# A planner's prices: engine times and GpSimd's hold in the simulated schedule of a two-block transformer kernel

## The chip, the cores and the metric

One core of a Trainium2 chip runs the whole program. The metric is the device time of one execution in microseconds; of the kernel before it is 4151.16 us, the median of three runs (4149.66 to 4156.11).

## The reference

Everything is float32, one sequence of 1024 tokens of width 1024, and a context of 256 tokens. The reference runs two different blocks one after the other:

```python
def reference(...):
    x = first_block(x, c, ctx, c_ctx, ...)   # two hybrid layers, then an RMS norm
    return second_block(x, p_2, ...)         # one layer of another kind
```

A layer of the first block normalizes and modulates the input, projects it (`h @ w_in`), and mixes three branches: attention with a latent key-value projection (6 heads), attention with grouped keys (6 heads, 2 key heads), both over the sequence and the context, and a gated depthwise convolution of 31 taps with a layer norm. The branches are gated, joined and multiplied by `w_out`. The second layer does not compute the context's output.

The second block computes a projection of 7896 columns; a gated linear attention in chunks; an indexer that scores keys, takes the 256 best of each query, and a sparse latent attention over them; their gated mix; a feed-forward part with a convolution of three taps; and a gated embedding. Three layer norms stand between.

## The kernel before

The kernel writes all of this as a list of small operations on tiles of 128 partitions by up to 512 columns, features on the partitions and tokens on the columns, in chunks of 512, 512 and 256 (context) tokens. For precision most operands are split in two halves of a reduced format: `hi` is a cast of the value (`copy`, line 293 of VectorE or line 284 of ACT), `lo` the rest (`lo`, a `tensor_tensor` subtraction, line 325 on VectorE or 327 on GpSimd), and a product is three matmuls (line 384): hi by hi, hi by lo and lo by hi. So nearly every matrix that TensorE reads has first passed through one cast and one subtraction.

Each operation (`Op`) has in `alts` the engines that can run it, each with a price in microseconds: `t` TensorE, `a` ACT, `v` VectorE, `p` GpSimd, `d` a DMA. Many casts can go to `a` or `v`, many subtractions, sums and products to `v` or `p`; the rest has one engine. GpSimd cannot read PSUM, so only operations on SBUF have `p`. `Plan.schedule` then simulates the engines with these prices: at each moment an engine that is free takes the ready operation of the lowest number (`pr`), and an operation with two engines is refused by the dearer one when the cheaper engine's remaining work, 0.6 us for each operation that stands ready there (at most 12), and its own price sum up to less than the price on the dearer one. The finish of an operation, its price and a fixed delay (`LAT`) make its readers ready. Buffers are handed out in the same simulation: 89 tiles of 128x512 in SBUF (`pg`), 8 PSUM banks (`ps`) and a few others. `Plan.merge` interleaves two lists of operations by the sum of their `t` prices.

What comes out is an order for each engine, which is emitted as it stands (`emit`). On the chip every engine works off its queue in this order; the simulation's times are gone, and an instruction that waits holds up all that follow it on its engine.

The stages in their order are: embedding, norm and modulation (to about 100 us), projections and convolution of layer 0, its two attentions, its output; the same for layer 1; indexer and scores; gated linear attention with the top-k search on VectorE beside it; its projection; the sparse attention; its projections; the feed-forward part; the gated embedding with the last layer norm.

The helpers with prices are `c_act` and `act` (ACT), `copy`, `c_v`, `c_p`, `tt` (sum, product, subtraction), `stt` and `ts` (VectorE with scalars), `scale`, `red` (maximum along a row), `mm` and `tr` (TensorE). For 512 columns of SBUF the old prices are 0.520 us on ACT, 0.600 for `tt` on VectorE and 1.225 on GpSimd, 0.660 for `stt`, 0.334 for a cast on VectorE, 0.216 for a matmul.

Of the kernel before, what the change touches and what calls it, by code (L numbers as in the profile page):

```python
# [4 lines left out]
F32 = mybir.dt.float32  # L5
# [110 lines left out]
class View:  # L116


    __slots__ = ("buf", "ap", "ops", "key")
# [42 lines left out]


class Op:
    __slots__ = ("alts", "reads", "writes", "emit", "idx", "succ", "npred", "allocs", "table", "bufs", "tag", "pr", "late")


BASIC = ("Copy", "Identity", "Square", "Abs", "Relu")
# [4 lines left out]
class Plan:  # L173
# [37 lines left out]
    def op(self, alts, reads, writes, emit, table=None):  # L211
        o = Op()
        o.alts = alts
        o.reads = [x for x in reads if isinstance(x, View)]
        o.writes = [x for x in writes if isinstance(x, View)]
        o.emit = emit
        o.table = table
        o.tag = self.tag
        o.late = self.late
        self.cur.append(o)  # L220
        return o
# [37 lines left out]
        return out  # L259

    def c_act(self, n, src, extra=0):
        return (n * 0.833 + (52 if isinstance(src, View) and src.psum else 93) + extra) / 1000

    def act(self, out, in_, func, bias=None, scale=1.0, accum=None, alts=None):
        nc = self.nc
# [31 lines left out]
    def copy(self, out, in_, engs="av"):  # L297
        a = {}
        n = out.n
        if "v" in engs:  # L300
            a["v"] = (n * (1.04 if in_.psum else 0.52) + 68) / 1000
        if "a" in engs:
            return self.act(out, in_, "Copy", alts=a)
        return self.op(a, [in_], [out], lambda e: self._copy(e, out, in_))
# [2 lines left out]
        return {"v": self.nc.vector, "p": self.nc.gpsimd}[e]  # L307

    def c_v(self, n, ex=0):
        return (n * 1.04 + 68 + ex) / 1000  # L310

    def c_p(self, n):
        return (n * 2.1 + 150) / 1000

    def tt(self, out, in0, in1, op, engs="v"):
        o = getattr(OP, op)
# [23 lines left out]
    def ts(self, out, in0, s1, s2, op0, op1=None, accum=None):  # L340
        o0 = getattr(OP, op0)
        k = {} if op1 is None else {"op1": getattr(OP, op1)}

        def emit(e):
            if accum is not None:
                k["accum_out"] = real(accum)
            self.nc.vector.tensor_scalar(out=real(out), in0=real(in0), scalar1=real(s1), scalar2=real(s2), op0=o0, **k)  # L347

        return self.op({"v": (out.n * (1.04 if in0.psum or accum is not None else 0.52) + 130 + (127 if accum is not None else 0)) / 1000},
                       [in0, s1, s2], [out, accum], emit)  # L350

    def scale(self, out, in_, col):

        n = out.n

        def emit(e):
            if e == "a":
                self.nc.scalar.activation(real(out), real(in_), AF.Copy, scale=real(col))
            else:
                self.nc.vector.tensor_scalar(out=real(out), in0=real(in_), scalar1=real(col), scalar2=None, op0=OP.mult)  # L360

        return self.op({"v": (n * (1.04 if in_.psum else 0.52) + 130) / 1000, "a": self.c_act(n, in_, 93)},
                       [in_, col], [out], emit)

    def red(self, out, in_, op="max"):
# [13 lines left out]

    def mm(self, out, lhsT, rhs, start, stop, cost=None):  # L380
        n = rhs.n
        c = cost or max(n * 1.676 if rhs.ap.dtype == F32 or n < 256 else n * 0.4219, 60) / 1000
        return self.op({"t": c}, [lhsT, rhs] + ([] if start else [out]), [out],
                       lambda e: self.nc.tensor.matmul(real(out), lhsT=real(lhsT), rhs=real(rhs), start=start, stop=stop))  # L384

    def tr(self, out, in_, ident):
        return self.op({"t": 0.109}, [in_, ident], [out],
                       lambda e: self.nc.tensor.transpose(real(out), real(in_), real(ident)))  # L388

    def dma(self, out, in_, cost=None):  # L390
# [10 lines left out]
    def schedule(self, window=1500, dwindow=1200, boost=0, queue=0.25, verbose=False):  # L401
# [8 lines left out]
        for o in ops:  # L410
            preds = set()
            bufs = {}
# [110 lines left out]
        while len(order) < N:  # L523
            progress = False
            for e in engs:
                while busy[e] <= now + 1e-9:
# [41 lines left out]
                    issued[o.idx] = True  # L568
                    progress = True
                    c = o.alts[e]  # L570
                    pre = None
                    if e == "a" and o.table is not None and o.table != table:
                        pre = o.table
# [1467 lines left out]
```

## Time and profile before

| | |
|---|---|
| median of 3 runs | 4151.16 us (4149.66 to 4156.11) |
| the profiled execution: time, span | 4150.0 us, 4148.1 us |
| TensorE busy, matmuls | 3908.4 us (94%), 18536 |
| VectorE busy, instructions | 3306.3 us (80%), 5640 |
| ACT busy, instructions | 2036.4 us (49%), 3969 |
| GpSimd busy, instructions | 1430.2 us (34%), 1257 |
| mean granted TensorE clock | 0.980 |

In the profile PE is TensorE's matmul, PEld its weight load, DVE VectorE, ACT ScalarE, POOL GpSimd. Matmuls overlap each other, so that a busy TensorE is not one at its peak. The mean length of an instruction is from its start to its end, also where the next one has started before that.

### The profile page before, as it was taken

What the parts mean: (1) busy time and instruction counts of PE and PEld (TensorE: products, weight loads), DVE (VectorE), ACT (ScalarE), POOL (GpSimd) and SP (SyncE); (2) the same over time, 40 slices, a digit from 0 to 9 for tenths busy, and PEclk for the clock granted to TensorE, in tenths of its full rate; (3) what the DMA queues carried; (4) which work ended last, traced back from release to release, by engine and by line L of the source; (5) the groups of instructions that cost most, each with busy time, mean ns of one, the idle gap of its engine ahead of it and who ended that gap; (6) DMA issues with size and microseconds to landing.
All of it is one profiled execution on the core that took longest, in us unless ns stands there. A gap on an engine that the chain in (4) does not pass through costs nothing. (4 is left out here: it accounts for less than half of the span.)

```text
span 4148.1 us, 54250 instructions
## 1 busy us (share of the span) xinstructions
PE 3908.4 (94%) x18536; PEld 3153.5 (76%) x18536; DVE 3306.3 (80%) x5640; ACT 2036.4 (49%) x3969; POOL 1430.2 (34%) x1257
## 2 busy tenths in 40 slices
PE   7989998989989998999999999999999999999988
PEld 4768766667877776778878878888878788888867
DVE  8995899997896789985999996388886865455588
ACT  5244576774334566763545551366663432222245
POOL 4542455663142344552223441011132411121153
PEclk8999999999999999999999999999999999999998
DMA  7132211123323110042111142100044411111121
GB/s 254 62 117 72 62 54 53 50 70 114 110 83 99 39 34 26 16 133 94 67 44 54 67 142 77 62 31 30 32 144 152 137 51 49 49 41 46 56 82 57
DMA packets 184981, 311.88 MB, mean 75 GB/s; under 512 B 22912, under 2 KB 46208, under 8 KB 184704
## 3 DMA queue, kind: packets, MB, share of 16 engines
q1 hardware_dynamic: 184704, 308.42, 23.0%
q8 instruction: 146, 2.39, 0.2%
q14 instruction: 131, 1.07, 0.1%
HBM read 237.81 MB, written 62.39 MB: 72 GB/s over the span
## 5 line engine op out<-in xcount | busy, mean ns | idle before, releaser
L384 PE MATMUL ps<-pg,pg 128*128 128x512 f32 (+4 forms) x17200 | 3843.6, 380 | 119.1 <-ACT pg L284 43.5
L384 PEld LDWEIGHTS ps<-pg,pg 128*128 128x128 f32 (+2 forms) x17200 | 3009.0, 190 | 798.5 <-ACT pg L284 72.9
L327 POOL TENSOR_TENSOR pg<-pg,pg 128x512 fp32r<-128x512 f32 (+4 forms) x935 | 1355.7, 1462 | 2338.7 <-ACT pg L284 1301.7
L284 ACT ACTIVATE pg<-pg 128x512 fp32r<-128x512 f32 (+9 forms) x1529 | 875.5, 601 | 893.5 <-DVE pg L335 240.6
L325 DVE TENSOR_TENSOR pg<-pg,pg 128x512 fp32r<-128x512 f32 (+8 forms) x1126 | 956.2, 868 | 218.7 <-ACT pg L284 162.6
L284 ACT ACTIVATE pg<-ps 128x512 f32<-128x512 f32 (+9 forms) x1351 | 686.8, 557 | 801.4 <-PE ps L384 597.4
L325 DVE TENSOR_TENSOR pg<-ps,pg 128x128 fp32r<-128x128 f32 (+9 forms) x690 | 381.3, 567 | 209.2 <-PE ps L384 146.3
L335 DVE SCALAR_TENSOR_TENSOR pg<-ux,c,pg 128x512 f32<-128x512 f32 x416 | 348.7, 867 | 9.6 <-ACT pg L284 2.2
L368 DVE TENSOR_REDUCE sm<-ps 128x1 f32<-128x512 f32 (+1 forms) x492 | 326.1, 679 | 9.6 <-PE ps L384 7.0
L293 DVE CAST pg<-pg 128x512 fp32r<-128x512 f32 (+4 forms) x387 | 226.9, 596 | 72.0 <-ACT pg L284 34.0
L284 ACT ACTIVATE pg<-ps,c 128x512 f32<-128x512 f32 (+1 forms) x182 | 127.3, 708 | 250.0 <-PE ps L384 218.5
L335 DVE SCALAR_TENSOR_TENSOR pg<-pg,c,pg 128x512 f32<-128x512 f32 (+3 forms) x242 | 220.1, 946 | 5.5 <-ACT pg L284 5.2
L388 PE MATMUL ps<-c,pg 128*128 128x128 f32 (+1 forms) x796 | 180.2, 274 | 14.3 <-DVE pg L293 5.8
L293 DVE COPY ux<-ps 128x512 f32<-128x512 f32 x83 | 57.3, 690 | 143.3 <-ACT pg L284 133.6
L1523 DVE MAX8 sm<-ux 128x8 f32<-128x384 f32 (+5 forms) x192 | 168.8, 887 | 3.3
L1524 DVE MATCH_REPLACE8 ux<-sm,ux 128x384 f32<-128x384 f32 (+5 forms) x192 | 167.7, 875 | 0.0
L384 PE MATMUL ps<-pg,c 128*128 128x512 f32 (+3 forms) x196 | 85.2, 502 | 74.9 <-DVE pg L325 28.6
L388 PEld LDWEIGHTS ps<-c,pg 128*128 128x128 f32 (+1 forms) x796 | 107.6, 141 | 40.3 <-issue 6.2
L284 ACT ACTIVATE pg<-pg,sm 128x512 f32<-128x512 f32 (+2 forms) x192 | 116.2, 606 | 11.2 <-DVE sm L347 10.7
L384 PEld LDWEIGHTS ps<-pg,c 128*128 128x128 f32 (+2 forms) x196 | 33.6, 176 | 105.7 <-DVE pg L325 31.6
L671 ACT ACT_TABLE_LOAD x84 | 107.8, 1283 | 1.5
L1778 DVE CUSTOM_DVE_ANT_0 pg<-ps,pg 128x512 f32<-128x512 f32 (+3 forms) x176 | 100.0, 575 | 8.5 <-PE ps L384 6.3
(74 smaller groups left out, 1017.2 us busy)
## 6 DMA issues: line engine op xcount, KB each, us to landing
d<-pg SPq DMA_DIRECT2D x202, 256.0 KB, 2.1
pg<-d SPq DMA_DIRECT2D x178, 256.0 KB, 3.3
pg<-in_w2a SPq DMA_DIRECT2D x108, 256.0 KB, 2.8
pg<-in_wmod SPq DMA_DIRECT2D x96, 256.0 KB, 3.1
pg<-in_wup SPq DMA_DIRECT2D x88, 256.0 KB, 2.7
pg<-in_win SPq DMA_DIRECT2D x80, 256.0 KB, 3.3
pg<-in_wout SPq DMA_DIRECT2D x64, 256.0 KB, 3.3
pg<-in_wdn SPq DMA_DIRECT2D x48, 256.0 KB, 2.7
```

What stands on the lines that cost most here:

```text
L284: nc.scalar.activation(real(out), real(in_), fn, scale=real(scale), **k)
L293: self.nc.vector.tensor_copy(real(out), real(in_))
L325: self.nc.vector.tensor_tensor(out=real(out), in0=real(in0), in1=real(in1), op=o)
L327: self.nc.gpsimd.tensor_tensor(out=real(out), in0=real(in0), in1=real(in1), op=o)
L335: self.nc.vector.scalar_tensor_tensor(out=real(out), in0=real(in0), scalar=real(scalar), in1=real(in1), op0=o0, op1=o1)
L368: lambda e: self.nc.vector.tensor_reduce(out=real(out), in_=real(in_), axis=AX.X, op=o))
L384: lambda e: self.nc.tensor.matmul(real(out), lhsT=real(lhsT), rhs=real(rhs), start=start, stop=stop))
L388: lambda e: self.nc.tensor.transpose(real(out), real(in_), real(ident)))
L671: nc.scalar.preload_act_table_set(pre)
L1523: P.vec(P.c_v(n), [w], [m8], lambda e, m8=m8, w=w: nc.vector.max(real(m8), real(w)))
L1524: P.vec(P.c_v(n), [w, m8], [w], lambda e, m8=m8, w=w: nc.vector.match_replace(real(w), real(m8), real(w), MARK))
L1778: lambda e, p=p, s=s, n=n, m=mk[t, b], a=sm[:, b:b + 1]: nc.vector.tensor_tensor_reduce(out=real(p), in0=real(s[:, 0:n]), in1=real(m), sca ...
```

## The change

The prices are replaced. For 512 columns they become 0.630 us on ACT from SBUF, 0.598 from PSUM, 0.687 for `tt` on VectorE, 1.326 on GpSimd, 0.747 for `stt`, 0.421 for a cast, 0.228 for a matmul; a transpose falls from 0.109 to 0.06. A new flag `dual` marks operations that VectorE can run, that read no PSUM and at least one tile of more than 64 columns of SBUF. When the simulation starts such an operation on VectorE while GpSimd is at work, it adds 0.42 us for each us of GpSimd's remaining work, up to the operation's price over 0.58. The choice between two engines still compares the plain prices. `LAT`, the priorities, the buffers and the operations stay.

```diff
 class Op:
-    __slots__ = ("alts", "reads", "writes", "emit", "idx", "succ", "npred", "allocs", "table", "bufs", "tag", "pr", "late")
+    __slots__ = ("dual", "alts", "reads", "writes", "emit", "idx", "succ", "npred", "allocs", "table", "bufs", "tag", "pr", "late")
...
+        o.dual = "v" in alts and not any(x.psum for x in o.reads) and sum(x.n > 64 for x in o.reads) > 0
...
     def c_act(self, n, src, extra=0):
-        return (n * 0.833 + (52 if isinstance(src, View) and src.psum else 93) + extra) / 1000
+        return (n * 0.836 + (170 if isinstance(src, View) and src.psum else 202) + extra) / 1000
...
-            a["v"] = (n * (1.04 if in_.psum else 0.52) + 68) / 1000
+            a["v"] = (n * (1.04 if in_.psum else 0.52) + 155) / 1000
...
     def c_v(self, n, ex=0):
-        return (n * 1.04 + 68 + ex) / 1000
+        return (n * 1.04 + 155 + ex) / 1000
 
     def c_p(self, n):
-        return (n * 2.1 + 150) / 1000
+        return (n * 2.2 + 200) / 1000
...
-        c = cost or max(n * 1.676 if rhs.ap.dtype == F32 or n < 256 else n * 0.4219, 60) / 1000
+        c = cost or max(n * 1.774 if rhs.ap.dtype == F32 or n < 256 else n * 0.4434 + 1, 60) / 1000
...
     def tr(self, out, in_, ident):
-        return self.op({"t": 0.109}, [in_, ident], [out],
+        return self.op({"t": 0.06}, [in_, ident], [out],
...
                     c = o.alts[e]
+                    if e == "v" and o.dual and busy["p"] > now:
+                        c += 0.42 * min(busy["p"] - now, c / 0.58)
```

`ts` and `scale` on VectorE go from 130 to 190 ns beside the columns in the same way.

The order has the same operations; 4463 of them can run on two engines, and 1371 of these now run on the other. By the numbers of the buffers that they write, 493 go from VectorE to GpSimd and 239 back, 370 from VectorE to ACT and 269 back. In sum VectorE's queue has 4901 operations for 5256, ACT's 3761 for 3660, GpSimd's 1507 for 1253. TensorE's 18512 and the 1400 DMAs are the same in number.

First place: the end of layer 0's attention with grouped keys. VectorE's queue before (in a name like pg2638_10097 the first number is the buffer's and is the same in both kernels, the second counts tiles in the order emitted; pg2638 is the low part of the probabilities pg2636, pg2637 their cast):

```order
L293 CAST pg2637_10072<-pg2636_10034 128x512
L293 CAST pg2641_10082<-pg2640_10048 128x512
L325 TENSOR_TENSOR pg2638_10097<-pg2636_10034,pg2637_10072 128x512
L325 TENSOR_TENSOR pg2642_10107<-pg2640_10048,pg2641_10082 128x512
L293 CAST pg2675_10117<-pg2674_10041 128x256
L325 TENSOR_TENSOR pg2675_10117<-pg2674_10041,pg2675_10117 128x256
L293 CAST pg2649_10128<-pg2648_10068 128x512
L325 TENSOR_TENSOR pg2678_10131<-pg2677_10080,pg2678_10131 128x256
L325 TENSOR_TENSOR pg2650_10146<-pg2648_10068,pg2649_10128 128x512
L293 CAST pg2661_10159<-pg2660_10111 128x512
L325 TENSOR_TENSOR pg2658_10167<-pg2656_10103,pg2657_10154 128x512
L325 TENSOR_TENSOR pg2662_10175<-pg2660_10111,pg2661_10159 128x512
```

and GpSimd's queue now, at the same place:

```order
L329 TENSOR_TENSOR pg2634_10023<-pg2632_9972,pg2633_10009 128x512
L329 TENSOR_TENSOR pg2638_10053<-pg2636_9982,pg2637_10044 128x512
L329 TENSOR_TENSOR pg2642_10070<-pg2640_10000,pg2641_10060 128x512
L329 TENSOR_TENSOR pg2675_10082<-pg2674_10029,pg2675_10082 128x256
L329 TENSOR_TENSOR pg2646_10104<-pg2644_10021,pg2645_10089 128x512
L329 TENSOR_TENSOR pg2678_10107<-pg2677_10042,pg2678_10107 128x256
L329 TENSOR_TENSOR pg2658_10141<-pg2656_10057,pg2657_10117 128x512
L329 TENSOR_TENSOR pg2662_10155<-pg2660_10073,pg2661_10126 128x512
```

Six subtractions of VectorE's run (of 2638, 2642, 2675, 2678, 2658, 2662) stand now on GpSimd, in one row with the two that it had before; the subtraction of 2650 stays on VectorE, and the casts of 2675, 2649 and 2661 went to ACT.

Second place: the last chunk of the gated embedding at the program's end, GpSimd's queue before (pg9707 is the sum of the outputs, pg9708 that of their squares, for the last layer norm; the other rows are products, and from pg9740 on the mean is subtracted):

```order
L327 TENSOR_TENSOR pg9708_39759<-pg9708_39759,pg9715_39765 128x256
L327 TENSOR_TENSOR pg9717_39771<-pg9718_39486,pg9717_39771 128x256
L327 TENSOR_TENSOR pg9725_39851<-pg9726_39555,pg9725_39851 128x256
L327 TENSOR_TENSOR pg9729_39868<-pg9730_39564,pg9729_39868 128x256
L327 TENSOR_TENSOR pg9707_39728<-pg9707_39728,pg9721_39846 128x256
L327 TENSOR_TENSOR pg9707_39728<-pg9707_39728,pg9725_39851 128x256
L327 TENSOR_TENSOR pg9708_39759<-pg9708_39759,pg9731_39911 128x256
```

and now:

```order
L329 TENSOR_TENSOR pg9707_39738<-pg9707_39738,pg9717_39725 128x256
L329 TENSOR_TENSOR pg9707_39738<-pg9707_39738,pg9721_39777 128x256
L329 TENSOR_TENSOR pg9707_39738<-pg9707_39738,pg9725_39820 128x256
L329 TENSOR_TENSOR pg9708_39744<-pg9708_39744,pg9719_39862 128x256
L329 TENSOR_TENSOR pg9708_39744<-pg9708_39744,pg9723_39870 128x256
L329 TENSOR_TENSOR pg9708_39744<-pg9708_39744,pg9727_39877 128x256
L329 TENSOR_TENSOR pg9729_39903<-pg9730_39622,pg9729_39903 128x256
L329 TENSOR_TENSOR pg9737_39929<-pg9738_39637,pg9737_39929 128x256
L329 TENSOR_TENSOR pg9708_39744<-pg9708_39744,pg9731_39932 128x256
L329 TENSOR_TENSOR pg9707_39738<-pg9707_39738,pg9733_39926 128x256
L329 TENSOR_TENSOR pg9707_39738<-pg9707_39738,pg9737_39929 128x256
```

Sums that alternated between VectorE and GpSimd now follow each other on GpSimd.

## Rows read from the trace of the kernel before

**Rows 1.** The page, part 1: busy us of each engine, share of the span, instructions
```profile
PE 3908.4 (94%) x18536; PEld 3153.5 (76%) x18536; DVE 3306.3 (80%) x5640; ACT 2036.4 (49%) x3969; POOL 1430.2 (34%) x1257
```

**Rows 2.** By stretch: start:end, length, then PE, PEld, DVE, ACT, POOL busy (count), PEclk, DMA
```profile
104.00:311.00 207.00, 178.93 (x891) 146.83 (x890) 206.01 (x282) 74.45 (x135) 103.60 (x62) 0.95 0.28 89
415.00:980.00 565.00, 511.04 (x2293) 387.35 (x2291) 533.34 (x815) 387.52 (x750) 331.62 (x286) 0.97 0.20 61
1141.00:1244.00 103.00, 90.75 (x403) 72.37 (x402) 101.69 (x127) 40.13 (x69) 51.56 (x26) 0.95 0.26 84
1340.00:1843.00 503.00, 468.67 (x2014) 353.80 (x2013) 447.92 (x699) 331.63 (x608) 252.14 (x245) 0.98 0.14 43
2017.00:2460.00 443.00, 419.30 (x2372) 362.00 (x2371) 424.61 (x779) 237.39 (x512) 167.15 (x144) 0.98 0.22 74
2460.00:2651.00 191.00, 191.00 (x844) 157.29 (x843) 106.88 (x141) 37.77 (x62) 33.25 (x26) 1.00 0.26 85
3960.00:4148.00 188.00, 150.43 (x786) 126.17 (x784) 166.82 (x229) 90.77 (x161) 90.92 (x67) 0.89 0.19 61
```

**Rows 3.** Timeline, one engine at a time: start, us, instructions of one kind in a row
```profile
147.19 26.57 DVE L335 SCALAR_TENSOR_TENSOR pg<-ux,c,pg 128x512 f32<-128x512 f32 x40
...
522.69 2.18 ACT L284 ACTIVATE pg<-pg 128x512 fp32r<-128x512 f32 x4
...
704.95 1.27 DVE L368 TENSOR_REDUCE sm<-ps 128x1 f32<-128x512 f32 x2
...
3701.80 10.37 PE L384 MATMUL ps<-pg,pg 128*128 128x512 f32 x44 [0.25 <-ACT pg L284]
```

**Rows 4.** Costliest groups, shapes apart: count, busy us, mean ns of one, idle before, releasers
```profile
L327 POOL TENSOR_TENSOR pg<-pg,pg 128x512 fp32r<-128x512 f32 x714 | 1085.7, 1531 | 1659.3 <-ACT pg L284 830.4 <-DVE pg L293 358.5 <-PE ps L384 293.8
L284 ACT ACTIVATE pg<-pg 128x512 fp32r<-128x512 f32 x972 | 591.7, 633 | 565.5 <-PE ps L384 153.0 <-DVE pg L325 141.0 <-DMA pg<-in_wup 49.7
L325 DVE TENSOR_TENSOR pg<-pg,pg 128x512 fp32r<-128x512 f32 x555 | 487.3, 891 | 128.8 <-ACT pg L284 90.7 <-PE ps L384 22.8 <-POOL pg L327 7.0
L335 DVE SCALAR_TENSOR_TENSOR pg<-ux,c,pg 128x512 f32<-128x512 f32 x416 | 348.7, 867 | 9.6 <-ACT pg L284 2.2
L325 DVE TENSOR_TENSOR pg<-pg,pg 128x512 f32<-128x512 f32 x271 | 245.4, 924 | 42.7 <-ACT pg L284 36.4 <-POOL pg L327 2.5
L335 DVE SCALAR_TENSOR_TENSOR pg<-pg,c,pg 128x512 f32<-128x512 f32 x192 | 189.5, 1013 | 5.5 <-ACT pg L284 5.2
L293 DVE CAST pg<-pg 128x512 fp32r<-128x512 f32 x297 | 184.2, 628 | 55.0 <-ACT pg L284 30.6 <-PE ps L384 18.6 <-DMA pg<-in_wout 3.5
L325 DVE TENSOR_TENSOR pg<-ps,pg 128x512 fp32r<-128x512 f32 x152 | 99.1, 684 | 23.6 <-ACT pg L284 23.0
L335 DVE SCALAR_TENSOR_TENSOR pg<-ps,c,pg 128x512 f32<-128x512 f32 x56 | 41.4, 745 | 21.8 <-PE ps L384 21.6
```

**Rows 5.** Timeline, 970 to 981 us: three of VectorE's rows, two of GpSimd's
```profile
970.25 1.40 DVE L325 TENSOR_TENSOR pg<-pg,pg 128x512 fp32r<-128x512 f32 x2
972.59 0.43 DVE L293 CAST pg<-pg 128x512 fp32r<-128x512 f32 x1
975.80 3.59 DVE L325 TENSOR_TENSOR pg<-pg,pg 128x512 fp32r<-128x512 f32 x3 [0.16 <-ACT pg L284]
...
975.38 1.41 POOL L327 TENSOR_TENSOR pg<-pg,pg 128x512 fp32r<-128x512 f32 x1 [1.08 <-ACT pg L284]
977.48 3.04 POOL L327 TENSOR_TENSOR pg<-pg,pg 128x512 fp32r<-128x512 f32 x2 [0.69 <-PE ps L384]
```

**Rows 6.** Waits: engine, line <- whom it waited for, us in total, times, longest
```profile
POOL pg L327 <- ACT pg L284: 1357.9, 308, 70.5
PEld ps L384 <- POOL pg L327: 63.1, 98, 6.3
```

**Rows 7.** Timeline near the end: GpSimd's and VectorE's 256-wide instructions
```profile
4105.21 3.39 POOL L327 TENSOR_TENSOR pg<-pg,pg 128x256 f32<-128x256 f32 x3 [2.04 <-DVE pg L325]
...
4107.09 0.93 DVE L325 TENSOR_TENSOR pg<-pg,pg 128x256 f32<-128x256 f32 x1 [0.62 <-POOL pg L327]
```

More of the change, by code (lines that the diff above doesn't have):

```diff
@@ L347, in emit @@
             self.nc.vector.tensor_scalar(out=real(out), in0=real(in0), scalar1=real(s1), scalar2=real(s2), op0=o0, **k)
-        return self.op({"v": (out.n * (1.04 if in0.psum or accum is not None else 0.52) + 130 + (127 if accum is not None else 0)) / 1000},
+        return self.op({"v": (out.n * (1.04 if in0.psum or accum is not None else 0.52) + 190 + (127 if accum is not None else 0)) / 1000},
                        [in0, s1, s2], [out, accum], emit)
@@ L360, in emit @@
                 self.nc.vector.tensor_scalar(out=real(out), in0=real(in_), scalar1=real(col), scalar2=None, op0=OP.mult)
-        return self.op({"v": (n * (1.04 if in_.psum else 0.52) + 130) / 1000, "a": self.c_act(n, in_, 93)},
+        return self.op({"v": (n * (1.04 if in_.psum else 0.52) + 190) / 1000, "a": self.c_act(n, in_, 93)},
                        [in_, col], [out], emit)
```

## The prediction, made before the changed kernel was run

> **What bounds the kernel now.** I read the page first, then a table by stretch, then single stretches of the timeline. TensorE is busy 3908.4 of 4148.1 us and VectorE 3306.3 [rows 1]; a mean over the program says little, so the table by stretch comes next [rows 2]. There the reader should see two kinds of stretch. In 2460 to 2651 us TensorE is busy all the time at a granted clock of 1.00 and VectorE barely half: nothing that VectorE does matters there. In six others (104 to 311, 415 to 980, 1141 to 1244, 1340 to 1843, 2017 to 2460, 3960 to 4148 us: the convolutions, both layers' attention, the top-k beside the gated linear attention, the end) VectorE is busy 1880 of 2009 us, TensorE idles 190 us (of 240 in the whole span), and the granted clock falls to 0.89 to 0.98. So VectorE's load there sets the time, and what the change does to it decides.
>
> **What the new prices are.** Rows of equal instructions back to back show the time that an engine gives to one [rows 3]: 40 convolution steps on VectorE take 26.57 us, 0.664 each; four ACT copies 2.18 us, so with the last one's full length of 0.63 the others take 0.52; two reductions 1.27 us, 0.60 for the first; 44 matmuls 10.37 us, 0.23 each. The groups [rows 4] give lengths instead: 0.867 for the first (with GpSimd's hold) and 0.633 for the second. An instruction starts some 0.08 to 0.11 us before the one ahead of it has ended. The old prices in the code were 0.660, 0.520, 0.600 and 0.216 us; the new ones are 0.747, 0.630, 0.687 and 0.228. So the new matmul price is right where the old was 5% low; the new prices of VectorE and ACT are lengths, and as the time for which the engine is taken they are 13 to 21% high, where the old were right but for the hold. The Trainium skill, page "Perfetto Trace Analysis", section "Optimizing Scalar/DVE Operations", says the same: profiled latency is about twice the engine-busy overhead, as its second half overlaps with the next instruction; the trace agrees (0.664 against 0.747).
>
> **GpSimd's hold is real.** Two subtractions of 128x512 without GpSimd beside them take 1.40 us; three take 3.59 us where GpSimd runs 0.99 and 1.91 us of that time [rows 5]. Alone they would take 0.60 + 0.60 + 0.69 = 1.89 us, so 1.70 us are lost in 2.90, 0.59 per us of GpSimd at most. Over the whole program: instructions that read SBUF twice, or cast from it, against those that read PSUM (0.684 and 0.745) or a cast alone (0.43) [rows 4, 5]: 555 x 0.207 + 271 x 0.240 + 416 x 0.122 + 192 x 0.268 + 297 x 0.198 = 341 us, over GpSimd's 1430 us busy [rows 1] 0.24 per us at least, as smaller groups are left out. The planner was blind to all this and thought VectorE faster than it is; now it thinks it slower than it is. The Trainium skill ("SBUF", section "Who interferes with whom") says that the loser is blocked for the whole instruction; that would be 1 per us, and the rows show at most 0.59. By its price the load term below would be a loss of 116 us.
>
> **The change, part by part.** Nothing computed changes. By buffer numbers, VectorE loses 355 instructions net, GpSimd gains 254 subtractions and products, ACT 101 copies; 157 and 68 of them lie in the six stretches (13 and 8, 40 and 34, 3 and 5, 30 and 16, 35 and 2, 36 and 3 in their order).
>
> 1. Taken from VectorE there: of the 254, 187 are 512 wide (0.60 us by rows 3), the others mostly 256 wide (0.33, half of the columns): 0.53 in the mean, 157 x 0.53 = 83 us. A cast from SBUF gives back about 0.35 (0.43 less 0.08), 68 x 0.35 = 24. Together 107 us.
>
> 2. Given to GpSimd: 1.531 us for 512 columns [rows 4], 1.13 for 256 (three in 3.39 us) [rows 7], 1.42 in the mean, 157 x 1.42 = 223 us more beside VectorE. The hold on it: 54 us at 0.24, 132 at 0.59. I take 0.33, nearer to the lower end since that one is a mean over the program, but above it since in these stretches GpSimd is busier (332 of 565 us in the longest) [rows 2]: 74 us. VectorE's load falls by 107 - 74 = 33 us; ends 53 less and 25 more. The tail is where it is worst: a sum of 256 columns takes 0.93 us beside GpSimd [rows 7], longer than one of 512 without it, and 36 more go over there, into sums that GpSimd now makes in a row (second place of the order).
>
> 3. Lateness. A low part that GpSimd makes lands after 1.53 instead of 0.89 us, and a matmul may wait for it. TensorE's weight loads wait for GpSimd 98 times, 63.1 us [rows 6], 0.065 us for each of the 972 sums, products and subtractions that the order gives GpSimd; 254 more make 16 us. Part of that falls where VectorE sets the pace anyway: +8, ends 0 and 16. The 101 ACT copies, and four more ACT table loads (85 rows to 89), are hidden: ACT is busy 388 of 565 us in the fullest stretch; were it full, they would cost their 0.52 us each on their chains.
>
> 4. Order. PE's queue is nearly the same stage by stage; inside the units it shifts. In the six stretches VectorE itself idles 2009 - 1880 = 129 us, while TensorE also waits: queues in a fixed order, behind a producer that is later than planned. With the old prices producers were late by the hold, with the new ones they are early by 0.08 to 0.11 us each, and a queue that expects its data late waits less. No row prices this: bounds are half of the 129 us gained, 65, and 40 lost. I take an eighth, 16 us gained, nearer to nothing, since most of what is planned stands as before.
>
> The profiled execution took 4150 us (span 4148.1): 4150 - 33 + 8 - 16 = 4109; the median of the runs lies 1 us above it, so **4110 us**.
>
> **The rivals.**
>
> *Late GpSimd operands (slower).* Prices that are too high for VectorE make the planner send to GpSimd even what a matmul needs next. For: at the first place of the order eight low parts stand in a row on GpSimd, which a matmul reads next. Each is 0.64 us later; the 33 us of step 2 are gone when 52 of the 254 are waited for. Now 1 in 10 is (98 of 972). At 1 in 2, 127 x 0.64 = 81 us: 4150 - 33 - 16 + 81 = 4182; without the gain of step 4 and with the hold's upper end 4256. Against: GpSimd mostly waits for its own inputs (1357.9 us for ACT alone) [rows 6], so it takes things as they come. A sentence of the Trainium skill ("Perfetto Trace Analysis", "Optimizing Scalar/DVE Operations") speaks for this: offloading between GpSimd and VectorE might not help, as they share a port.
>
> *Order was the trouble (a larger gain).* If the matching of plan and chip is what TensorE lacked, half of its 190 us of idle time in the six stretches goes, with the clock behind it: 4150 - 33 - 65 = 4052 or below. For: the clock is under 1.00 in each of them [rows 2]. Against: VectorE is 94 to 99% busy in three, and order does not shorten a full engine.
>
> *Nothing comes of it.* The engine choice changes, but at a hold of 107/223 = 0.48 per us VectorE's load stays, and lateness and order cancel: 4150. For: 0.48 lies between the two ends of rows 4 and 5.
>
> **How the numbers follow.** A measurement of this kernel can tell 0.2%, 8 us, from no change. Forecast (4060 to 4142 us) 0.44, larger gain 0.20, nothing 0.12, slower 0.24. So faster 0.64, same 0.12, slower 0.24. The range goes from 4045, which leaves out some 0.08 of the larger gain, to 4180, which leaves out some 0.11 of the slower case. The forecast's own range is 4060 to 4142.
>
> **What would show it.** Right: VectorE's busy time falls by some 60 to 150 us, GpSimd's rises by about 350, and TensorE's idle time in 415 to 980 and 2017 to 2460 us shrinks while the stretch from 2460 on keeps its length. GpSimd's 128x512 mean stays about 1.5 us. Step 2 is wrong if VectorE's busy time hardly falls or the mean of its 128x512 subtraction rises over 1.0 us; step 3 if TensorE's waits for GpSimd go far over 63 + 16 us; step 4 if TensorE's idle time falls by much more or less than VectorE's load. The last 188 us should not get shorter. The prediction fails as a whole if the stretches that VectorE does not bound change by more than a few us, for then order alone was at work.

## The result, and the profile after

The changed kernel takes 4053.27 us (median of 4 runs, 4049.64 to 4054.66), the kernel before on the same chip 4150.41 us: a ratio of 0.976 [0.975, 0.978], 97 us gained. The forecast was 4110 us. The time lies within the stated range (4045 to 4180 us) but below the forecast's own (4060 to 4142), 1 us from the 4052 us of the rival "Order was the trouble"; how much of that hit is luck is said below.

The page of the changed kernel, part 1, beside [rows 1]:

```profile
span 4052.6 us, 54435 instructions
## 1 busy us (share of the span) xinstructions
PE 3878.6 (96%) x18536; PEld 3138.1 (77%) x18536; DVE 3236.8 (80%) x5285; ACT 2077.8 (51%) x4074; POOL 1755.2 (43%) x1511
```

The span is 95.5 us shorter. TensorE's idle time fell from 239.7 to 174.0 us, which is 65.7 of them; its busy time for the same 18536 matmuls fell by 29.8, while the mean granted clock rose from 0.980 to 0.987. VectorE's busy time fell by 70 and GpSimd's rose by 325, both about as forecast.

The table by stretch of the changed kernel, cut where TensorE has done as many matmuls as at the borders of [rows 2] (columns as there):

```profile
108.00:289.00 181.00, 172.85 (x893) 142.30 (x892) 175.14 (x214) 76.67 (x136) 105.85 (x69) 1.00 0.30 100
391.00:944.00 553.00, 509.05 (x2294) 382.70 (x2293) 509.60 (x737) 396.96 (x779) 377.45 (x321) 0.98 0.21 62
1109.00:1205.00 96.00, 88.35 (x401) 71.33 (x400) 87.61 (x102) 41.23 (x72) 58.32 (x28) 0.96 0.30 94
1295.00:1775.00 480.00, 458.01 (x2014) 351.72 (x2013) 434.94 (x657) 334.26 (x625) 299.77 (x279) 1.00 0.15 47
1948.00:2362.00 414.00, 412.01 (x2371) 359.52 (x2370) 374.31 (x693) 232.44 (x502) 187.22 (x174) 1.00 0.23 76
2362.00:2552.00 190.00, 190.00 (x842) 156.62 (x841) 135.34 (x183) 45.54 (x77) 46.64 (x36) 1.00 0.27 92
3867.00:4053.00 186.00, 147.76 (x785) 123.65 (x783) 170.07 (x189) 97.08 (x168) 138.85 (x103) 0.90 0.19 62
```

The six stretches that the prediction called bound by VectorE (all but the sixth row) take 1910 us instead of 2009: the whole gain. VectorE's load in them falls by 128 us, from 1880 to 1752, though over the whole program only by 70. Outside the six it is busy 59 us longer (1485 us, 1426 before): that work has gone elsewhere in time, not to another engine. Part of it is in the sixth row: VectorE is busy 135 us there, not 107 [rows 2], and the stretch is no longer for it, as TensorE sets its pace.

What moved can be counted. Two views show the rounds of the top-k search (one MAX8 each) in the stretch of the gated linear attention and in the one behind it (the fifth and the sixth row); before:

```profile
L1523 DVE MAX8 sm<-ux 128x8 f32<-128x512 f32 (+4 forms) x158 | 127.8, 817 | 2.4
...
L1523 DVE MAX8 sm<-ux 128x8 f32<-128x1024 f32 (+1 forms) x34 | 41.0, 1212 | 0.8
```

and after the change:

```profile
L1527 DVE MAX8 sm<-ux 128x8 f32<-128x384 f32 (+4 forms) x142 | 109.5, 783 | 0.8
...
L1527 DVE MAX8 sm<-ux 128x8 f32<-128x1024 f32 (+1 forms) x50 | 57.4, 1170 | 0.4
```

Sixteen rounds, 18 us of MAX8 and about as much for the replacement that follows each, left the full stretch for one with room. The steps of the first convolution did the same: 171 of them lie in the first row's stretch before, 128 after, and right behind it VectorE is busy 92 of 102 us, where it was busy 60 of 104.

The costliest groups of the changed kernel, shapes apart, of GpSimd and VectorE, and the largest waits of TensorE's weight loads:

```profile
L329 POOL TENSOR_TENSOR pg<-pg,pg 128x512 fp32r<-128x512 f32 x862 | 1294.8, 1517 | 1443.5 <-ACT pg L286 801.5 <-PE ps L386 287.6 <-DVE pg L295 235.3
...
L327 DVE TENSOR_TENSOR pg<-pg,pg 128x512 fp32r<-128x512 f32 x407 | 415.8, 1032 | 89.9 <-ACT pg L286 56.9 <-PE ps L386 19.8 <-POOL pg L329 9.0
L337 DVE SCALAR_TENSOR_TENSOR pg<-ux,c,pg 128x512 f32<-128x512 f32 x416 | 362.6, 898 | 22.2 <-ACT pg L286 13.9 <-POOL pg L329 0.9
...
L327 DVE TENSOR_TENSOR pg<-pg,pg 128x512 f32<-128x512 f32 x232 | 228.6, 1003 | 32.4 <-ACT pg L286 27.2 <-DMA pg<-pg 2.0
L337 DVE SCALAR_TENSOR_TENSOR pg<-pg,c,pg 128x512 f32<-128x512 f32 x192 | 204.8, 1094 | 7.7 <-ACT pg L286 7.6
L295 DVE CAST pg<-pg 128x512 fp32r<-128x512 f32 x258 | 188.4, 737 | 30.3 <-ACT pg L286 19.8 <-PE ps L386 3.2 <-POOL pg L329 2.0
L327 DVE TENSOR_TENSOR pg<-ps,pg 128x512 fp32r<-128x512 f32 x152 | 97.7, 683 | 22.1 <-ACT pg L286 21.2 <-issue 0.7
```

```profile
PEld ps L386 <- POOL pg L329: 95.2, 140, 8.9
PEld ps L386 <- ACT pg L286: 57.5, 78, 10.5
PEld ps L386 <- DVE pg L327: 44.3, 46, 5.3
...
PEld ps L386 <- DVE pg L295: 16.6, 19, 2.1
```

GpSimd's price is what it was (1.517 us, 1.531 before). VectorE's instructions on SBUF got longer again (0.891 to 1.032 us for the subtraction, 0.628 to 0.737 for the cast), those on PSUM did not (0.683). TensorE's weight loads wait for GpSimd 32 us more than in [rows 6], and for the others less; their waits before were:

```profile
PEld ps L384 <- ACT pg L284: 90.2, 81, 8.7
PEld ps L384 <- DVE pg L325: 73.2, 81, 8.7
...
PEld ps L384 <- DVE pg L293: 50.0, 41, 6.1
```

### The profile page after: what moved, and what is told of

Same layout as the page of the kernel before. It is cut to its first block, busy times and chain, and to the rows that moved or that the text cites. A ratio compares the mean times of both kernels' runs of the same rounds, so it can differ in the third digit from the quotient of the medians.

```text
span 4052.6 us, 54435 instructions
## 1 busy us (share of the span) xinstructions
PE 3878.6 (96%) x18536; PEld 3138.1 (77%) x18536; DVE 3236.8 (80%) x5285; ACT 2077.8 (51%) x4074; POOL 1755.2 (43%) x1511
## 5 line engine op out<-in xcount | busy, mean ns | idle before, releaser
L386 PE MATMUL ps<-pg,pg 128*128 128x512 f32 (+4 forms) x17200 | 3800.6, 378 | 95.6 <-ACT pg L286 26.3
L386 PEld LDWEIGHTS ps<-pg,pg 128*128 128x128 f32 (+3 forms) x17200 | 2989.0, 189 | 771.5 <-POOL pg L329 63.5
L329 POOL TENSOR_TENSOR pg<-pg,pg 128x512 fp32r<-128x512 f32 (+5 forms) x1173 | 1670.0, 1442 | 1841.6 <-ACT pg L286 991.2
L286 ACT ACTIVATE pg<-pg 128x512 fp32r<-128x512 f32 (+5 forms) x1609 | 912.3, 598 | 783.3 <-DVE pg L337 240.0
L286 ACT ACTIVATE pg<-ps 128x512 f32<-128x512 f32 (+12 forms) x1365 | 686.0, 550 | 829.1 <-PE ps L386 648.2
L327 DVE TENSOR_TENSOR pg<-pg,pg 128x512 fp32r<-128x512 f32 (+8 forms) x888 | 857.2, 979 | 143.6 <-ACT pg L286 97.9
L295 DVE CAST pg<-pg 128x512 fp32r<-128x512 f32 (+3 forms) x310 | 219.2, 714 | 41.7 <-ACT pg L286 19.8
L337 DVE SCALAR_TENSOR_TENSOR pg<-pg,c,pg 128x512 f32<-128x512 f32 (+3 forms) x242 | 235.2, 1010 | 7.9 <-ACT pg L286 7.6
L390 PE MATMUL ps<-c,pg 128*128 128x128 f32 (+1 forms) x796 | 163.6, 272 | 11.5 <-DVE pg L295 5.9
L380 POOL MEMSET pg<- 128x128 f32 (+2 forms) x213 | 52.3, 266 | 169.9 <-PE ps L386 107.7
```

Of the source, the lines that this page charges most:

```text
L286: nc.scalar.activation(real(out), real(in_), fn, scale=real(scale), **k)
L295: self.nc.vector.tensor_copy(real(out), real(in_))
L327: self.nc.vector.tensor_tensor(out=real(out), in0=real(in0), in1=real(in1), op=o)
L329: self.nc.gpsimd.tensor_tensor(out=real(out), in0=real(in0), in1=real(in1), op=o)
L337: self.nc.vector.scalar_tensor_tensor(out=real(out), in0=real(in0), scalar=real(scalar), in1=real(in1), op0=o0, op1=o1)
```

## The experiments

Every kernel here computes the same thing. Gains are differences of medians to the kernel before on the same chip; lines of a kernel with an edit ahead of them are shifted.

**Choice or order?** The first two take the two halves of the change apart: a table of bits (`TOOK`, taken from the other kernel's plan) fixes which engine each two-engine operation gets, and the prices then decide the order alone.

```diff
+        if len(alts) > 1:
+            e = "v" if TOOK[self.took] == "1" else [x for x in alts if x != "v"][0]
+            alts = {e: alts[e]}
+            self.took += 1
```

The changed kernel's choice, with the prices of before:

> Every operation runs on the engine that the changed kernel gives it, but the order comes from the old prices without the hold. Load (the gain is that VectorE has 355 instructions less): most of the 97 us stays, 4050 to 4085 us. Order (the gain is when VectorE's own long jobs, the convolutions, the top-k and the second modulation, take their place between the urgent casts and subtractions): most is lost, 4115 to 4150 us.

The choice of before, with the new prices and the hold:

> Every operation runs on the engine that it had before, the order comes from the new prices and the hold. Load: 4120 to 4150 us. Order: 4055 to 4090 us, though VectorE keeps its 5256 instructions.

Measured: the choice alone 4160 us, ratio 1.003 [1.002, 1.004], 11 us lost; the order alone 4068 us, 0.981 [0.979, 0.982], 81 us gained. So the load that the prediction built on earns nothing by itself, and the order earns four fifths of everything. With the new order in place the choice adds 16 us (97 against 81), which is no more than an edit without meaning can move (17 us, below). The stretches of the choice alone (the sixth row of [rows 2] left out):

```profile
108.00:326.00 218.00, 185.31 (x893) 153.22 (x892) 215.71 (x286) 79.70 (x143) 124.12 (x75) 0.92 0.27 86
427.00:987.00 560.00, 509.32 (x2293) 387.53 (x2292) 497.83 (x740) 400.25 (x784) 362.77 (x322) 0.97 0.20 62
1148.00:1255.00 107.00, 92.49 (x404) 74.71 (x403) 106.18 (x124) 42.06 (x73) 63.82 (x30) 0.92 0.25 79
1350.00:1847.00 497.00, 469.27 (x2014) 350.25 (x2013) 420.47 (x654) 335.54 (x624) 290.09 (x276) 0.99 0.14 44
2021.00:2468.00 447.00, 423.18 (x2373) 366.89 (x2372) 421.14 (x754) 241.23 (x514) 192.54 (x177) 0.97 0.21 72
...
3968.00:4158.00 190.00, 148.11 (x785) 124.16 (x783) 162.25 (x190) 93.37 (x166) 134.94 (x103) 0.90 0.18 59
```

and of the order alone:

```profile
106.00:283.00 177.00, 172.48 (x892) 142.75 (x891) 169.96 (x226) 66.42 (x124) 94.88 (x59) 1.00 0.31 101
383.00:959.00 576.00, 523.83 (x2292) 394.60 (x2291) 529.74 (x813) 385.88 (x755) 324.96 (x291) 0.95 0.20 60
1120.00:1213.00 93.00, 87.93 (x403) 70.38 (x402) 87.68 (x107) 38.66 (x66) 47.59 (x26) 0.98 0.29 94
1304.00:1791.00 487.00, 462.54 (x2013) 350.21 (x2012) 449.65 (x701) 326.99 (x611) 260.18 (x250) 1.00 0.15 45
1964.00:2379.00 415.00, 412.82 (x2374) 360.89 (x2373) 374.58 (x714) 218.27 (x481) 154.24 (x137) 1.00 0.22 74
...
3891.00:4067.00 176.00, 145.48 (x786) 122.92 (x784) 161.83 (x229) 92.78 (x163) 96.19 (x67) 0.92 0.20 65
```

With the choice alone VectorE's load in the six falls by 56 us (1824), their length rises by 10: VectorE idles 195 us in them instead of 129, and the planner, which now thinks VectorE relieved, filled it with long jobs: 195 convolution steps in the first stretch instead of 171, 162 top-k rounds instead of 158. With the order alone nothing leaves VectorE's queue, yet its load in the six falls by 107 us, the length by 85: 123 steps, 139 rounds. Over the whole program its busy time falls by 33 of these 107 us (3273 after 3306), as the same instructions got a little shorter; the rest lies outside the six.

**Which price?** One part of the change each: the hold alone; the lengths of ACT, VectorE and GpSimd alone; the matmul's and transpose's price alone; and hold and matmul price together, with the old lengths.

```diff
+                    if e == "v" and o.dual and busy["p"] > now:
+                        c += 0.42 * min(busy["p"] - now, c / 0.58)
```

> The kernel before with the hold alone: all old prices. True (the gain comes from a simulation that knows what VectorE really has to do): the hold is the larger half of what was missing, so 4070 to 4100 us. Dear (any price that makes VectorE look fuller helps, the more the better): about half of the gain, 4090 to 4115 us.

> The kernel before with the new prices of VectorE, ACT and GpSimd, without the hold and with the old matmul price. True: these prices are lengths, not the time for which an engine is taken, so they make the simulation right only in the mean; 4100 to 4150 us. Dear: about half of the gain, 4085 to 4115 us.

> The kernel before with the new, longer matmul and shorter transpose price alone. Those prices are closer to what rows show, but a dearer matmul lets the simulation place fewer of them between maker and reader: medians 20, 17 and 14. Distance: slower than before, 4155 to 4190 us. A simulation that is right in more prices is better: 4130 to 4150 us.

> The hold and the new matmul price, but for VectorE, ACT and GpSimd the old prices, which are what back-to-back rows show as the time taken. True: as good as the change or better, 4030 to 4060 us. Dear: worse than the change by the missing part, 4080 to 4115 us.

And the changed kernel with the VectorE prices that the change set (`copy`, `c_v`, `ts`, `scale`) 87 ns higher still:

```diff
-        return (n * 1.04 + 155 + ex) / 1000
+        return (n * 1.04 + 242 + ex) / 1000
```

> The changed kernel with every VectorE price another 87 ns higher, so 29% over the time taken for 512 columns. True: too much work leaves VectorE and the long jobs come late, 4065 to 4110 us. Dear: 4020 to 4050 us.

Measured: hold alone 0.983 [0.981, 0.984], 72 us gained; lengths alone 0.985 [0.984, 0.987], 62; matmul alone 1.015 [1.013, 1.016], 57 lost; hold and matmul 0.993 [0.991, 0.994], 31 gained; dearer still 0.988 [0.986, 0.990], 50 gained. Added up, the three parts give 77 us against 97, and the hold and the matmul price 15 against 31; differences of 20 and 16 us are about what 1 ns on one price can move (17 us, below), so no interplay of the parts is shown. The new price that the rows called right, the matmul's (0.23 us taken in [rows 3], 0.216 before, 0.228 now; in that run with the transpose's), does harm. The two that were put together because the rows support both give less than the hold alone.

**Distance, or long jobs out of turn?** Two theories of the order. One: a longer planned latency from every producer to TensorE gives late operands room (the figures are us):

```diff
-        "a": dict(t=0.27, ...), "v": dict(t=0.26, ...), "p": dict(t=0.2, ...)
+        "a": dict(t=1.27, ...), "v": dict(t=1.26, ...), "p": dict(t=1.20, ...)
```

> The kernel before with all its old prices; only the simulation's delay from ACT, VectorE or GpSimd to TensorE is 1.0 us longer. That changes almost no engine choice (5276 for 5256 on VectorE) and leaves the long jobs where they were, but puts more matmuls in TensorE's queue between the last one that an operand depends on and the first that reads it: median 28, 31 and 30 in the gated linear attention and the two grouped-key attentions, for 22, 19 and 18 before and 33, 28 and 28 with the change. Distance (queues in fixed order stall because a reader stands too close behind its maker): 4070 to 4100 us. Long jobs (their place is what counts): 4140 to 4155 us. Load: 4150 us.

> The same with 2.0 us more: medians 34, 37 and 34. Distance: as good as the change or a little behind, 4050 to 4090 us. Long jobs and load: 4140 to 4160 us.

> The changed kernel with the delay to TensorE 1.0 us longer: medians 38, 32 and 33, VectorE 4994 for 4901. Distance: there is enough of it already, within 15 us of 4053, better if anything. Long jobs, load: 4045 to 4065 us.

Measured: 0.999 [0.998, 1.000] and, with 2 us, 1.006 [1.004, 1.007] in the kernel before; 0.980 [0.979, 0.982] in the changed one, 14 us worse than without, which is less than an edit without meaning can move. Distance is not what was lacking.

The other: VectorE's long jobs (both convolutions, the modulation, the top-k: work that no matmul reads soon) are taken before their turn. They are held back in the kernel before, to 30 operations ahead of TensorE, or pushed ahead in the changed one:

```diff
+            if e == "v" and len(o.alts) == 1 and o.tag in ("conv0", "conv1", "topk", "mod1") and o.idx > max(front[0], head) + 30:
+                return False
```

> The kernel before with its old prices; only, in the simulation VectorE may not start an operation of its long jobs (convolutions, top-k, second modulation) more than 30 operations ahead of where TensorE stands in the list. Load: 4150 us, as the engines' shares hardly change (5214 for 5256 on VectorE). Order: the long jobs no longer push the urgent work back, 4060 to 4100 us.

```diff
+            if "v" in o.alts and len(o.alts) == 1 and o.tag in ("conv0", "conv1", "topk", "mod1"):
+                o.pr -= 1000
```

> The changed kernel, but the long jobs on VectorE get a priority as if they stood 1000 operations earlier, so that they run ahead as they did before. Load: 4050 to 4070 us, VectorE has 4901 instructions still. Order: 4110 to 4160 us.

Measured: held back 1.006 [1.005, 1.008], 23 us lost; pushed ahead 0.998 [0.997, 0.999], 8 gained, so nearly all of the 97 us are gone. This edit goes further than undoing the change: 197 convolution steps lie in the first stretch, 171 before. What it does is seen in the timelines of VectorE, ACT and TensorE of that kernel:

```profile
139.49 18.64 DVE L337 SCALAR_TENSOR_TENSOR pg<-ux,c,pg 128x512 f32<-128x512 f32 x28
158.04 0.69 DVE L327 TENSOR_TENSOR ux<-ps,pg 128x512 f32<-128x512 f32 x1
158.65 1.41 DVE L337 SCALAR_TENSOR_TENSOR pg<-ux,c,pg 128x512 f32<-128x512 f32 x2
...
162.14 3.40 DVE L337 SCALAR_TENSOR_TENSOR pg<-ux,c,pg 128x512 f32<-128x512 f32 x5
165.45 0.41 DVE L349 TENSOR_SCALAR pg<-pg,c,c 128x256 f32<-128x256 f32 x1
...
165.96 0.42 ACT L286 ACTIVATE pg<-pg 128x256 fp32r<-128x256 f32 x1 [15.42 <-DVE pg L349]
...
139.65 12.75 PE L386 MATMUL ps<-pg,pg 128*128 128x512 f32 x65
166.43 0.80 PE L386 MATMUL ps<-pg,pg 128*128 128x256 f32 x2 [14.03 <-ACT pg L286]
```

TensorE has stood still for 14 us when its matmul starts at 166.43. Its operand is the cast on ACT at 165.96, which waited 15 us for the instruction of VectorE at 165.45, and that one stands behind the convolution steps in VectorE's queue. A fixed limit does not help the kernel before: the convolution leaves the first stretch (108 steps), but VectorE is then busy only 153 us of 190 there, and the program outside the six takes 2172 us instead of 2139, 18 of the 33 right behind that stretch (122 us instead of 104).

**What the prices really set.** What the gains so far follow best is neither a single price nor its truth, but VectorE's planned load over TensorE's (the sums of the prices along the plan). Two kernels test that without touching VectorE's prices in the one, or undoing them in the other: the kernel before with every matmul 15% cheaper, and the changed one with every matmul 25% dearer.

```diff
-        c = cost or max(n * 1.676 if rhs.ap.dtype == F32 or n < 256 else n * 0.4219, 60) / 1000
+        c = (cost or max(n * 1.676 if rhs.ap.dtype == F32 or n < 256 else n * 0.4219, 60) / 1000) * 0.85
```

> The kernel before, with every matmul price times 0.85 and nothing else touched (VectorE's old prices, no hold). VectorE's planned load over TensorE's goes from 0.754 to 0.862, the ratio that the changed kernel has (0.863). Ratio theory (what counts is how loaded the planner thinks VectorE is beside TensorE, since that decides how much spare time it believes VectorE has for jobs that nobody waits for): 4055 to 4095 us, as fast as the hold alone or faster. Accuracy theory (plans get better as single prices get nearer to the chip's): the matmul price moves from 5 per cent low to 19 per cent low, so slower than 4150. Scatter theory (any change of prices throws the dice anew): anywhere in 4080 to 4210.

> The changed kernel, with every matmul price times 1.25: new VectorE, ACT and GpSimd prices and the hold stay. VectorE's planned load over TensorE's falls from 0.863 to 0.712, below the kernel before (0.754). Ratio theory: the whole gain goes, 4150 to 4220 us. Accuracy theory: worse than the changed kernel, but the hold and VectorE's prices still help: 4070 to 4120. Scatter theory: anywhere.

The same two kernels with 1 ns more on one price (68 to 69, 155 to 156) show what an edit without meaning does:

> The kernel before with 1 ns more on VectorE's price of a two-operand instruction (68 to 69 ns): a change of 0.1 per cent that means nothing and still reorders the queues. Ratio and accuracy theory: 4140 to 4160 us. Scatter theory: 20 us or more from 4150.

> The changed kernel with 1 ns more on VectorE's price of a two-operand instruction (155 to 156 ns). Ratio and accuracy theory: 4043 to 4063 us. Scatter theory: 20 us or more from 4053.

Measured: cheap matmul 4058 us, 0.978 [0.976, 0.979], 92 gained; dear matmul 4227 us, 1.018 [1.017, 1.020], 76 lost, 7 us more than the theory of the ratio allowed; shaken 0.999 [0.998, 1.000] and 0.973 [0.971, 0.974], 5 us from the kernel before and 17 from the changed one. One line that makes the matmul price too low by a fifth (0.183 us against 0.23) thus gives nearly the gain of the whole change, and one that makes it too high by nearly a quarter (0.285) takes more than all of it away. By planned load ratio, with the gain in us, all kernels of this section:

```
0.706 choice alone    -11    0.757 before, 1 us later   6    0.862 cheap matmul        92
0.712 dear matmul     -76    0.761 before, 2 us later -22    0.863 the change          97
0.725 matmul alone    -57    0.761 hold+matmul         31    0.864 pushed ahead         8
0.751 held back       -23    0.791 hold alone          72    0.867 change, shaken     114
0.751 before, shaken    5    0.801 long jobs dearer    63    0.877 change, 1 us later  84
0.754 before            0    0.824 the rest dearer     45    0.902 order alone         81
                             0.851 lengths alone       62    0.938 dearer still        50
```

The small steps mean little (an edit without meaning moves 5 and 17 us). The rise as a whole does mean something: 173 us from 0.712 to 0.863. That the gain falls again behind 0.9 rests on one kernel. The ratio is not all either: choice alone lies 65 us above its neighbour at 0.712, two kernels at 0.761 are 53 us apart, and pushing the long jobs ahead takes 89 us away at an unchanged ratio. So the ratio acts through the order that the planner makes of it: another order at the same ratio has another time. The cheap matmul's stretches look like those of the change:

```profile
104.00:282.00 178.00, 170.25 (x895) 143.86 (x894) 173.78 (x228) 73.67 (x132) 81.44 (x61) 1.00 0.33 105
385.00:937.00 552.00, 507.54 (x2295) 388.65 (x2294) 519.62 (x769) 396.75 (x785) 333.13 (x294) 0.97 0.21 62
...
1950.00:2365.00 415.00, 411.48 (x2370) 359.81 (x2369) 379.49 (x718) 230.82 (x501) 168.93 (x153) 1.00 0.23 77
2365.00:2555.00 190.00, 190.00 (x843) 156.68 (x842) 135.90 (x183) 45.61 (x78) 40.88 (x33) 1.00 0.27 90
```

**Long jobs or the rest?** The last two raise the ratio in the kernel before by one kind of VectorE's work at a time, when it is started and not when an engine is chosen:

```diff
                     c = o.alts[e]
+                    if e == "v" and len(o.alts) == 1 and o.tag in ("conv0", "conv1", "topk", "mod1"):
+                        c *= 1.35
```

> The kernel before, where the planner lets only VectorE's long jobs (both convolutions, the modulation, the top-k: work that no matmul reads soon) take 1.35 times their old price once they are chosen. Every other price stays as before. The long jobs then stand about where the changed kernel has them (the middle one of the first convolution behind the 1075th matmul in the plan; before 907, changed 1099; of the top-k 9935; 9719 and 9949). VectorE's planned load over TensorE's: 0.801. Place theory (the gain comes from the long jobs standing later among the others in VectorE's queue): 4055 to 4085 us. Load theory (it comes from the other instructions being thought longer): 4130 to 4160.

> The kernel before, where the planner lets VectorE's other instructions, all but the long jobs, take 1.18 times their old price once they are chosen. VectorE's planned load over TensorE's: 0.824, between the kernels with the hold alone (0.791) and with the lengths alone (0.851), but the long jobs stay nearly where the kernel before has them (928th matmul for the first convolution, 9781st for the top-k). Place theory: 4115 to 4150 us. Load theory: 4070 to 4095.

Measured: long jobs dearer 0.985 [0.984, 0.987], 63 gained; the rest dearer 0.990 [0.988, 0.992], 45. Neither theory holds alone, and both times lie outside the ranges of both. Each kind gives a share; the 18 us between them are about what 1 ns on one price can move, so which is larger stays open. What they do in the six stretches, with the others (us; lengths and VectorE's busy time from their tables by stretch; VectorE's time on long jobs in the six; convolution steps in the first stretch, top-k rounds in the fifth). The last two columns are TensorE's idle time between 90 us and its last matmul, while VectorE runs a long job and otherwise. They, and the time on long jobs, come from matching VectorE's instructions in the trace one by one to the operations of the plan (the short value loads of the top-k left out):

```
                             ---- the six ----                  TensorE idle
                     gain  length  busy  long   steps rounds  beside long  else
before                  0    2009  1880   544     171    158           43   160
the change             97    1910  1752   479     128    142           21   111
order alone            81    1924  1773   465     123    139           20   111
cheap matmul           92    1919  1774   475     131    144           16   129
long jobs dearer       63    1936  1745   462     127    141           23   135
the rest dearer        45    1955  1803   521     163    153           31   139
change, pushed ahead    8    1994  1804   548     197    142           76   123
choice alone          -11    2019  1824   579     195    162           46   154
before, held back     -23    1997  1793   482     108    147           47   158
dear matmul           -76    2067  1904   580     185    163           64   175
```

VectorE's load in the six does not order the gains: 1793 us go with 23 lost, 1803 with 45 gained. TensorE's idle time beside a long job parts them: 16 to 31 us in the five kernels that gain 45 us or more, 43 to 76 in the others. The held-back kernel fits: its long jobs left the six, but 15 of its 47 us lie outside, where they now stand in the way.

Nine of the eighteen kernels came out outside every definite range given for them (choice alone, held back, matmul alone, hold and matmul, before with 2 us, dear matmul, the change shaken, and the last two). The theories fit the direction better than the size, and held back fits neither.

## Why the prediction was wrong

**The step that failed is step 4, the order.** It was put at 16 us gained, at most 65, "nearer to nothing, since most of what is planned stands as before"; by itself it is worth 81 us. Load and lateness together, put at 25 us gained (33 less 8), are 11 lost by the choice alone. The premise that VectorE's load in the six sets their time fails with it: the choice alone takes 56 us off that load, and the six get 10 us longer. The argument against its rival, that "order does not shorten a full engine", was the mistake: order does not make an engine's work less, but it decides in which stretch the work is done. The prediction counted what leaves VectorE inside the six stretches by engine choice alone, and forgot what leaves them in time. With the new prices the planner thinks VectorE more loaded beside TensorE (0.863 for 0.754), finds less spare time on it, and starts fewer long jobs ahead of the operands that TensorE waits for; they end up where VectorE has over a third of its time free (before, it is busy 60 of 104 us behind the first stretch and 107 of 191 behind the fifth). VectorE spends 544 us on long jobs in the six stretches before and 479 after; outside them 148 and 232. The total time outside the six hardly changes (2139 and 2143 us).

**Only part of it is a direct collision.** Of TensorE's idle time between 90 us and its last matmul, 43 of 203 us lie beside a long job on VectorE before, 21 of 133 after. So 22 of the 71 us are matmuls that stood still while a long job ran. The other 49 are not the long jobs' place alone: when these are pushed ahead in the changed kernel, the idle time beside them rises by 55 us, that elsewhere only by 12. Delays passed on through the queues would explain them, but no run here shows how they come about. Nor is it settled why VectorE itself idles more in the six in every other kernel of the table than before (129 us): 145 to 204, most with the jobs held back.

**The number of the rival.** "Order was the trouble" gave 4052 us, 1 us from the result, but not by its own reasoning. It speaks of half of TensorE's 190 us of idle time, which is 95, and its sum takes half of VectorE's 129, 65; its 33 us of load are not what the choice brought. Its condition, a plan that matches the chip better, is not what gained either: the prices nearest to the rows gained 31 us, a matmul price a fifth too low 92. That order counted was right; the hit was luck. Of the full stretches held against it ("94 to 99% busy in three") there are four by [rows 2].

**Step 1 and step 2, the load.** The amounts held: VectorE's busy time fell by 70 us (60 to 150 asked for), GpSimd's rose by 325 (about 350). The hold, over the program: 407 x 0.348 + 232 x 0.319 + 416 x 0.153 + 192 x 0.349 + 258 x 0.307 = 425 us over GpSimd's 1755, 0.24 per us as before, and 84 us more for 325 us more of GpSimd, 0.26; both are lower ends, as smaller groups are left out, so the 0.33 taken for the six is not refuted. But as a cause of the gain the step fell: the choice alone takes 56 us off VectorE in the six and loses 11. That the subtraction's mean went over 1.0 us (1.032) was named as a sign against the step. By that sign the step is wrong, by the load it is not; more of what is left running beside GpSimd would explain both, which no run here separates.

**Step 3, lateness.** Waits of the weight loads for GpSimd rose by 32 us, not by at most 16. It was outweighed: those for ACT and for VectorE's two largest lines fell by 33, 29 and 33. So the mechanism of the slower rival is there, with 32 us of waiting where its price was 81.

**The other signs.** The stretch from 2460 us kept its length (191 and 190 us), the last 188 became 186, TensorE's idle time in the stretch of the gated linear attention went from 23.7 to 2.0 us, and in the longest one from 54 to 44. Two signs would have misled: TensorE's idle time fell by 66 us and VectorE's load by 70, by which step 4 would stand; and the time outside the six stayed, by which the order would not be what was at work. The prediction saw that producers "were late by the hold" in the old plan, and that the new prices are too high as times taken; it did not see that too high is what this planner needed, up to a point. Even prices nearer to the rows are no remedy: the old lengths, which the rows call right, with the hold and the better matmul price, gained 31 us.

## What to carry to other kernels

When a planner's prices change, look at which long, unhurried jobs change their stretch in each engine's order before counting what changes its engine: here 107 us less load on VectorE in the six stretches went with 85 us less time (order alone), 128 with 99 (the change). Where a fixed limit moved it, 87 us went with 12, so ask also what the moved work collides with. In this planner the prices act as weights, and the ratio between two engines' loads counts for much, so a price that is nearer to the trace can be worse; tuning one ratio over a few values can be a cheaper search than measuring each price. Shake a price by 1 ns to learn how far two plans must differ before their difference means anything: here 5 us for one plan and 17 for the other.

## What the runs showed beside

GpSimd's hold on VectorE came out the same in both kernels: at least 0.24 us lost per us of GpSimd's work at 1430 and at 1755 us of it, while VectorE's 512-column subtractions that read PSUM kept their 0.68 us. The granted clock was lower where TensorE idled more: in the first stretch 0.95 with 28 us idle of 207, 1.00 with 8 of 181. And the fastest kernel here, the change with 156 for 155 in one price, takes 4036 us, 0.973 [0.971, 0.974], 17 below the change itself: a find of chance, not of design.
